# A hybrid diffusion layer on one core: gate rows on ScalarE's queue, deferred statistics, separate PSUM pools, earlier loads of w_down, later output stores

## The chip, the cores and the metric

The kernel runs on one core of a Trainium2 chip. The metric is the device time of one execution in microseconds, the median of several. A core has TensorE (PE: matmuls, with its weight loads listed apart as PEld), VectorE (DVE), ScalarE (ACT), GpSimd (POOL) and SyncE (SP), which computes nothing and issues DMAs. ACT and POOL can issue DMAs too. Every engine executes its own list of instructions strictly in order; an instruction that waits holds up everything behind it on its engine. Waits are on semaphores that other engines or finished DMAs raise.

## What is computed

One layer of a network: 128 context tokens and 2048 latent tokens of width 1024 pass a gated short convolution and a bidirectional mLSTM scan in chunks of 128 tokens, then a feed-forward part with a convolution, all in float32.

```python
def trunk_layer(x, mod, ...):
    h = rmsnorm(x, norm1) * (1 + scale1) + shift1
    z = h @ w_in
    sc_b, sc_c, sc_x, q, k, v, o, g = jnp.split(z, idx, axis=-1)
    u = (sc_c * sc_x).reshape(B, rows, row_len, D_CONV)
    y_sc = sc_b * conv3(u, conv_sc_w, conv_sc_b, axis=2).reshape(B, T, D_CONV)
    h_m, C, n, m = mlstm_bidir(heads(q), heads(k), heads(v), gates, C0, n0, m0)
    h_m = h_m * lax.rsqrt(jnp.mean(h_m * h_m, axis=-1, keepdims=True) + EPS)
    ...
    x = x + gate1 * (jnp.concatenate([y_sc, h_m], axis=-1) @ w_out)
    h2 = rmsnorm(x, norm2) * (1 + scale2) + shift2
    up = (h2 @ w_up).reshape(B, rows, row_len, 2 * D_FF)
    up = conv3(up, conv_ffn_w, conv_ffn_b, axis=ffn_axis).reshape(B, T, 2 * D_FF)
    a, gg = jnp.split(up, 2, axis=-1)
    x = x + gate2 * ((jax.nn.silu(gg) * a) @ w_down)
    return x, C, n, m
...
y_prompt = rmsnorm(xp, final_norm)
y_sample = rmsnorm(xs, final_norm)
```

## The kernel before

Tokens stand in the columns of every tile, features in the partitions. A float32 product is made of three matmuls of split operands: each matrix is a rounded high part and the rest (`wh`, `wl` for weights, `hH`, `hL` or `tH`, `tL` for activations), and `wh*hH + wh*hL + wl*hH` is summed in PSUM. ACT makes the high parts, DVE the low ones. The tokens of the first half are six blocks of 384 or 256 columns in three groups, (0,1), (2,3) and (4,5). `gemm` (L201) makes one 128-row piece of a product for one block: 8 x 3 matmuls into a PSUM tile `acc`.

The program runs through these stages. Python generators (`chain`, `run`, `islice`) decide which piece of side work is emitted between which two gemms; the framework then fixes the order of every engine's list and puts in the waits.

- The modulation vectors and the products with `w_in` (to about 640 us). Beside them `prep_down` (L576) forms sums of the blocks of `w_down` for a seven-product (Strassen-like) scheme: a lot of 512 or 384 columns is two loads `wm` (L586), four DVE operations (L601 to L604) and four stores to `wD` (L606). There are 12 lots. All three tiles of a lot come from one ring of five buffers, `wm`.
- The gates, then two passes of `weave` (L908) over the mLSTM units with gemms between them. A `Mix` unit is a chunk and a pair of heads: `load` (L828) fetches k, v, q, o, `sb` and the gate rows `R` (L834, one row of `nD` broadcast to all partitions, 512 KB, four buffers); `first` (L842) makes the scores S on PE (L845), adds a mask to R on DVE (L846), takes the exponential on ACT (L850) and multiplies with S on DVE (L854); `second` (L857) makes y on PE (L868, L870), from it `hv` on DVE, and squares it on ACT (`sj`, L887); `third` (L893) transposes hv on PE into the PSUM tile `st` (L897), scales it on DVE (o, L899) and stores it to `yD` (L902). There are 34 units. At step i of `weave` unit i runs `first`, unit i-3 `third`, unit i-1 `second`, and unit i+2 is loaded. Between two units lie one or two gemms.
- In the second pass these gemms are the short convolution (L418 to L439) and the output projection `out_proj` (L446): per group and per m of eight, weights `wst` (L109), rows of x (L466), a gemm for either block, the residual `row` on DVE (L483), its store to `xD` (L485), squares `sq` on ACT (L492) and their sum on DVE (L493). After a group its `stats` (L441) run: `inv_rms` (L124) multiplies the squares with ones on PE (L128, into a tile of the same pool `st`), and DVE (rc, L131) and POOL (L132) make 1/rms of it.
- `sums` applies the second norm to a pair of blocks (F, L234 to L253, tD). The third group's `out_proj` (`last`, L957) is run in between.
- The products with `w_up` in the seven-product scheme (PE L1143 to L1145, to about 2190 us), with PSUM tiles of three kinds, a, b and c, from one pool `pu` (L969); then those with `w_down` (PE L1201 to L1203). Their weights are loaded into `st` (L285, L294, L328). Finished blocks of the output are normed: `norm` (L1081) makes the 1/rms, spreads it, scales eight tiles (DVE L1091), stores them (`out_y`, L1093 for the second half of the tokens, L1095 for the first) and loads the next half's residual into the same tiles (L1060).

Nearly all DMAs are issued by SP (`Q` in the code), among them all those named here. `S` is ACT, `V` DVE, `G` POOL.

## Time and profile before

| | us |
|---|---|
| median of 3 runs | 2519.47 (2518.98 to 2521.13) |
| the profiled execution | 2520.55 |
| its span in the trace | 2518.8 |
| PE busy | 2464.3 (98%) |
| DVE busy | 1740.9 (69%) |
| ACT busy | 1100.6 (44%) |
| POOL busy | 67.0 (3%) |
| DMA, mean over the span | 201 GB/s |

The profile lists, for every instruction, its start, its duration and how long its engine stood idle before it, with the instruction or DMA that ended this idle time. A matmul's listed duration is longer than the step from one to the next, since they are pipelined. PEclk is the granted clock of TensorE: 1.00 in a stretch is its full level, 2.4 GHz, and 0.5 the lower one, 1.2 GHz. Times of the trace count from the start of the span.

### The profile page before, as it was taken

How to read it: one execution, taken by the hardware profiler on the slowest of the kernel's cores; microseconds unless marked ns; L12 is line 12 of the kernel's file. 1: busy time of each engine (PE TensorE's matmuls, PEld its weight loads, DVE VectorE, ACT ScalarE, POOL GpSimd, SP SyncE). 2: the span in 40 equal slices, each digit the busy share in tenths (PEclk: the TensorE clock that was granted, in tenths of full speed). 3: DMA queues.
4: the chain of work that ended last, by engine and by line, in shares of the span. 5: the costliest groups of instructions: out<-in, count | busy, mean ns of one | idle time of the engine just before them, and what ended most of it. 6: DMA issues, size and time to landing. Idle time of an engine off the chain costs nothing.

```text
span 2518.8 us, 46131 instructions
## 1 busy us (share of the span) xinstructions
PE 2464.3 (98%) x17967; PEld 2446.1 (97%) x17967; DVE 1740.9 (69%) x3401; ACT 1100.6 (44%) x2109; POOL 67.0 (3%) x130
## 2 busy tenths in 40 slices
PE   8999999999999989999999999999999999999998
PEld 8999999999999989999999999999999999999998
DVE  4995443343467767889798879776767787677665
ACT  4521143333344444555454446544545543443343
POOL 0000000000011110000000000000000000000000
PEclk9999999999999999999999999999999999999999
DMA  8888733466567886977456446544444485576544
GB/s 287 281 278 268 224 102 105 140 205 211 175 199 205 256 272 199 291 249 250 149 198 210 151 158 229 186 155 157 149 163 143 158 299 202 189 241 221 181 158 145
DMA packets 252445, 506.29 MB, mean 201 GB/s; under 512 B 22963, under 2 KB 153155, under 8 KB 241347
## 3 DMA queue, kind: packets, MB, share of 16 engines
q1 hardware_dynamic: 252226, 503.35, 60.5%
q8 instruction: 141, 2.31, 0.4%
q14 instruction: 78, 0.63, 0.1%
HBM read 355.24 MB, written 148.03 MB: 200 GB/s over the span
## 4 chain that ended last, share of the span: by engine, by line
PE 77%; DVE 9%; DMA 9%; issue 2%; ACT 2%; SPq 1%; POOL 0%; DVEq 0%; ACTq 0%; POOLq 0%
PE pa L1143 7%; PE pa L1145 7%; PE pa L1144 7%; PE acc L206 5%; PE acc L208 5%; PE acc L207 5%; PE pb L1145 3%; PE pb L1143 3%; PE pb L1144 3%; DVE jk L555 3%; PE pa L1203 2%; PE pa L1201 2%; PE pa L1202 2%; DMA wD<-wm 2%; DMA R<-nD 2%; PE pc L1144 2%
## 5 line engine op out<-in xcount | busy, mean ns | idle before, releaser
L206 PE MATMUL acc<-hH,wh 128*128 128x384 f32 (+1 forms) x1536 | 513.7, 334 | 5.5 <-DVE cr L425 3.0
L208 PE MATMUL acc<-hH,wl 128*128 128x384 f32 (+1 forms) x1536 | 504.9, 329 | 0.0
L207 PE MATMUL acc<-hL,wh 128*128 128x384 f32 (+1 forms) x1536 | 504.2, 328 | 0.0
L1143 PE MATMUL pa<-tH,wh 128*128 128x272 f32 x1408 | 409.2, 291 | 4.1 <-DVE row L483 2.9
L1145 PE MATMUL pa<-tH,wl 128*128 128x272 f32 x1408 | 407.9, 290 | 0.0
L1144 PE MATMUL pa<-tL,wh 128*128 128x272 f32 x1408 | 405.9, 288 | 0.0
L278 ACT ACTIVATE wh<-st 128x512 fp32r<-128x512 f32 (+1 forms) x312 | 188.7, 609 | 418.9 <-PE pa L1144 118.2
L206 PEld LDWEIGHTS acc<-hH,wh 128*128 128x128 f32 x1536 | 290.3, 189 | 7.5 <-DVE cr L425 3.4
L207 PEld LDWEIGHTS acc<-hL,wh 128*128 128x128 f32 x1536 | 290.1, 189 | 0.7
L208 PEld LDWEIGHTS acc<-hH,wl 128*128 128x128 f32 x1536 | 290.1, 189 | 0.3 <-issue 0.2
L984 DVE SCALAR_TENSOR_TENSOR tt<-raw,fw,tt 128x127 f32<-128x127 f32 (+4 forms) x264 | 242.2, 947 | 47.3 <-ACT tt L990 46.2
L279 DVE TENSOR_TENSOR wl<-st,wh 128x512 fp32r<-128x512 f32 (+1 forms) x312 | 205.4, 660 | 98.8 <-ACT wh L278 93.3
L1143 PEld LDWEIGHTS pa<-tH,wh 128*128 128x128 f32 x1408 | 265.7, 189 | 5.1 <-DVE row L483 3.1
L1144 PEld LDWEIGHTS pa<-tL,wh 128*128 128x128 f32 x1408 | 266.1, 189 | 0.0
L1145 PEld LDWEIGHTS pa<-tH,wl 128*128 128x128 f32 x1408 | 265.4, 189 | 0.0
L1143 PE MATMUL pb<-tH,wh 128*128 128x272 f32 x704 | 203.6, 289 | 0.4 <-ACT wh L278 0.4
L1145 PE MATMUL pb<-tH,wl 128*128 128x272 f32 x704 | 203.6, 289 | 0.0
L1144 PE MATMUL pb<-tL,wh 128*128 128x272 f32 x704 | 202.7, 288 | 0.0
L278 ACT ACTIVATE wh<-s 128x512 fp32r<-128x512 f32 x176 | 110.9, 630 | 148.1 <-PE pc L1144 90.5
L1203 PE MATMUL pa<-tH,wl 128*128 128x256 f32 (+1 forms) x528 | 152.6, 289 | 0.2 <-DVE wl L279 0.2
L1201 PE MATMUL pa<-tH,wh 128*128 128x256 f32 (+1 forms) x528 | 152.8, 289 | 0.0
L1202 PE MATMUL pa<-tL,wh 128*128 128x256 f32 (+1 forms) x528 | 152.4, 289 | 0.0
(236 smaller groups left out, 5485.3 us busy)
## 6 DMA issues: line engine op xcount, KB each, us to landing
st<-in_w_up SPq DMA_DIRECT2D x88, 512.0 KB, 4.5
wst<-in_w_in SPq DMA_DIRECT2D x48, 512.0 KB, 4.2
wU<-s SPq DMA_DIRECT2D x22, 1024.0 KB, 6.6
s<-wU SPq DMA_DIRECT2D x22, 1024.0 KB, 5.7
st<-wD SPq DMA_DIRECT2D x32, 704.0 KB, 4.9
st<-in_w_down SPq DMA_DIRECT2D x28, 704.0 KB, 4.1
R<-nD SPq DMA_DIRECT2D x34, 512.0 KB, 5.6
wm<-in_w_modr SPq DMA_DIRECT2D x32, 512.0 KB, 4.9
```

What stands on the lines that cost most here:

```text
L206: PE.matmul(acc[:, :n], w_h, hH[:, k, :n], start=(k == 0), stop=False)
L207: PE.matmul(acc[:, :n], w_h, hL[:, k, :n], start=False, stop=False)
L208: PE.matmul(acc[:, :n], w_l, hH[:, k, :n], start=False, stop=(k == KT - 1))
L278: S.activation(wh[:, :n], a, AF.Copy)
L279: V.tensor_sub(wl[:, :n], a, wh[:, :n].bitcast(F32))
L984: V.scalar_tensor_tensor(o, i, w, o, op0=ALU.mult, op1=ALU.add)
L1143: PE.matmul(acc, wh[:, w], rh, start=(kk == 0 and i in (0, 1, 5)), stop=False, skip_group_check=True)
L1144: PE.matmul(acc, wh[:, w], rl, start=False, stop=False, skip_group_check=True)
L1145: mm = PE.matmul(acc, wl[:, w], rh, start=False, stop=(kk == 3), skip_group_check=True)
L1201: PE.matmul(acc[p], wh[:, k], th[:, t], start=(c == kk == 0), stop=False, skip_group_check=True)
L1202: PE.matmul(acc[p], wh[:, k], tl[:, t], start=False, stop=False, skip_group_check=True)
L1203: PE.matmul(acc[p], wl[:, k], th[:, t], start=False, stop=(c == 2 and kk == nk - 1), skip_group_check=True)
```

## The change

There are five edits.

1. `Mix.load` issues R on ACT's DMA queue (`S.dma_start`) and not on SP's.
2. `out_proj` no longer runs a group's `stats` at its end. It puts them into a list `late`, from which the next group's `out_proj` takes them after its first gemm of m = 1, tied behind that gemm's last matmul (`latest`). Those of the last group still run beside the first products with `w_up`. In connection with this the last group runs four gemms, not one, ahead of the second part of `sums`.
3. The products with `w_up` and `w_down` take their PSUM tiles from three pools, c, b and a, not from one.
4. `prep_down` loads a lot ahead of the one whose sums it makes, and the tile of the sums has a ring `ws` of its own (2 buffers) beside `wm` (5).
5. `norm` stores a tile of the output, and reloads it, when two more have been scaled. For the second half's first block the two half stores of a tile become one.

```diff
@@ gemm
+    latest, late = [], []
...
-            PE.matmul(acc[:, :n], w_l, hH[:, k, :n], start=False, stop=(k == KT - 1))
+            mm = PE.matmul(acc[:, :n], w_l, hH[:, k, :n], start=False, stop=(k == KT - 1))
+        latest[:] = [mm]
@@ out_proj
                         acc = gemm(w, y, n)
+                        if m == 1 and b == grp[0] and late:
+                            with tc.issue_after(latest[0].ins):
+                                late.pop()()
...
-                if grp is grps[-1] and defer is not None:
-                    defer.append(lambda: stats(grp, sss))
-                else:
-                    stats(grp, sss)
+                late.append(lambda grp=grp, sss=sss: stats(grp, sss))
@@ prep_down
-                for mp, c0, n in lots:
-                    a, b = load(mp, c0, n)
+                nxt = load(*lots[0])
+                yield
+                for x, (mp, c0, n) in enumerate(lots):
+                    a, b = nxt
+                    if x + 1 < len(lots):
+                        nxt = load(*lots[x + 1])
                     store()
                     yield
                     a11, a12, a21, a22 = a[:, 0], a[:, 1], b[:, 0], b[:, 1]
-                    s = stp.tile([P, 1024], F32, name="wm", bufs=5).rearrange("p (k c) -> p k c", k=2)[:, :, :n]
+                    s = stp.tile([P, 1024], F32, name="ws", bufs=2).rearrange("p (k c) -> p k c", k=2)[:, :, :n]
@@ Mix.load
-                Q.dma_start(self.R.rearrange("p h k d t -> p (h k d t)"),
+                S.dma_start(self.R.rearrange("p h k d t -> p (h k d t)"),
                             nD[r0:r0 + 2].rearrange("h k d t -> (h k d t)")[None, :].to_broadcast([P, 1024]))
@@ the last group
-        late = []
-        last = out_proj(((4, 5),), late)
-        run(islice(last, 1))
+        last = out_proj(((4, 5),))
+        run(islice(last, 4))
@@ the products
-        pu = ph2.enter_context(tc.tile_pool(name="pu", bufs=2, space=PSUM))
+        pu = {k: ph2.enter_context(tc.tile_pool(name="p" + k, bufs=n, space=PSUM)) for k, n in (("c", 2), ("b", 2), ("a", 3))}
...
-            return pu.tile([P, 512], F32, name="p" + kind, bufs=3 if kind == "a" else 2)
+            return pu[kind].tile([P, 512], F32, name="p" + kind)
@@ norm
+            due = []
             for m in range(KT):
                 q = outs[m, blk][:, p * n:(p + 1) * n]
                 V.scalar_tensor_tensor(q, q, nrm[:, 2, m:m + 1], rb[:, :n], op0=ALU.mult, op1=ALU.mult)
-                if hf:
+                if then is None:
                     Q.dma_start(O["y"][m][:, t0 + p * n:t0 + (p + 1) * n], q)
-                elif p:
-                    Q.dma_start(O["y"][m][:, t0:t0 + 2 * n], outs[m, blk])
-                    then(m)
+                    continue
+                if p:
+                    due.append((m, outs[m, blk]))
                 if m % 2:
                     yield
+                    while len(due) > (2 if m < KT - 1 else 0):
+                        m1, o = due.pop(0)
+                        Q.dma_start(O["y"][m1][:, t0:t0 + 2 * n], o)
+                        then(m1)
```

In the order of the instructions this looks as follows. Line numbers of the changed kernel are up to 11 higher than those of the kernel before.

SP's list before, around the R load of one of the last units. `row` is a row of x for the residual, `k`, `q`, `v`, `o` and `sb` are the loads of `Mix`, `yD` is the store of `third`:

```order
L765 DMA q_10001<-qD 128x2x128 [waits DMAHW2_49]
L466 DMA row<-in_x 128x384 [waits DMAHW5_49,DMAHW3_49,Activation_49]
L902 DMA yD<-o_9511 128x2x128 [waits DMAHW4_49,DVE_49]
L834 DMA R<-nD 128x1024 [waits PE_49]
L770 DMA v_9999<-vD 128x258 [waits DMAHW6_49]
L765 DMA o_9961<-oD 128x2x128 [waits DMAHW7_49,DMAHW4_49]
L838 DMA sb<-sD 128x516 [waits DMAHW0_49,DVE_49]
```

ACT's list in the changed kernel around two of these loads (L857 is the exponential, L894 and L898 are `sj` and the scaling of hv, L111 makes a high part of `w_out`, L498 squares):

```order
L841 DMA R<-nD 128x1024 [waits DMAHW1_49,PE_49]
L894 ACTIVATE sj,hss<-hv 128x128 [waits DVE_49] x2
L898 ACTIVATE hv<-hv,hss 128x128 [waits Activation_49,Pool_49]
L898 ACTIVATE hv<-hv,hss 128x128 [waits Activation_49]
L111 ACTIVATE wh<-wst 128x1024 [waits PE_49]
L498 ACTIVATE sq<-row 128x384 [waits DVE_49]
L857 ACTIVATE R<-R,cols 128x128 [waits DMAHW1_49]
L857 ACTIVATE R<-R,cols 128x128 x3
L498 ACTIVATE sq<-row 128x384 [waits DMAHW2_49,DVE_49]
L841 DMA R<-nD 128x1024 [waits DMAHW6_49,PE_49]
```

The R load has left SP's list, where it stood behind the store of o, and stands on ACT behind the exponential of the unit before and ahead of `sj`.

PE's list before at the statistics of group (0,1), directly behind the y of a unit:

```order
L870 MATMUL y<-v_9654,R 128x129
L868 MATMUL y<-sb,qs 128x129
L870 MATMUL y<-v_9654,R 128x129
L128 MATMUL st<-ones,ss 128x1 [waits DVE_49]
L128 MATMUL st<-ones,ss 128x1 x2
L206 MATMUL acc<-hH,wh 128x384
L207 MATMUL acc<-hL,wh 128x384
```

PE's list in the changed kernel at the same statistics:

```order
L210 MATMUL acc<-hH,wl 128x384
L128 MATMUL st<-ones,ss 128x1 [waits DVE_49]
L128 MATMUL st<-ones,ss 128x1 x2
L208 MATMUL acc<-hH,wh 128x384
L209 MATMUL acc<-hL,wh 128x384
L210 MATMUL acc<-hH,wl 128x384
L208 MATMUL acc<-hH,wh 128x384
L128 MATMUL st<-ones,ss 128x1 [waits DVE_49]
L128 MATMUL st<-ones,ss 128x1 x2
L209 MATMUL acc<-hL,wh 128x384
```

DVE's list before at the two `rc` that read these statistics (`st` has one buffer, so the second block's `inv_rms` needs the first block's `rc` done):

```order
L493 TENSOR_TENSOR ss<-ss,sq 128x384 [waits Activation_49]
L877 TENSOR_SCALAR hv<-y,den 128x128 [waits DVE_49]
L131 TENSOR_SCALAR rc<-st 128x3 [waits PE_49,Pool_49]
L878 SCALAR_TENSOR_TENSOR hv<-y,den,hv 128x128 [waits DVE_49]
L131 TENSOR_SCALAR rc<-st 128x3 [waits PE_49,Pool_49]
```

DVE's list in the changed kernel there (L853 is the mask of a later unit):

```order
L885 SCALAR_TENSOR_TENSOR hv<-y,den,hv 128x128 [waits DVE_49]
L114 TENSOR_TENSOR wl<-wst,wh 128x512
L853 TENSOR_TENSOR R<-R,maskN 128x2x256 [waits DMAHW6_49]
L131 TENSOR_SCALAR rc<-st 128x3 [waits PE_49,Pool_49]
L489 SCALAR_TENSOR_TENSOR row<-acc,modT,row 128x384
L131 TENSOR_SCALAR rc<-st 128x3 [waits PE_49,Pool_49]
```

On PE the first block's statistics have moved behind a whole gemm; the second block's now stand four matmuls behind the first block's, where before they stood 15 matmuls behind. On DVE a low part of weights and a mask, which waits for its R to land, have come to stand ahead of the first `rc`.

SP's list before at the norm of the first half's second block, from its last store of the output to the next weights and activations:

```order
L1095 DMA out_y<-o_23312 128x512 [waits DVE_49]
L1060 DMA o_25930<-xD 128x576 [waits DMAHW7_49,DMAHW3_49]
L1060 DMA o_25934<-xD 128x576 [waits DMAHW4_49,DMAHW0_49]
L1060 DMA o_25938<-xD 128x576 [waits DMAHW5_49,DMAHW1_49]
L1060 DMA o_25942<-xD 128x576 [waits DMAHW6_49,DMAHW2_49]
L328 DMA st<-in_w_down 128x1408 [waits Activation_49]
L328 DMA st<-in_w_down 128x1408 [waits DVE_49]
```

The same place in the changed kernel:

```order
L1108 DMA out_y<-o_23318 128x512 [waits DVE_49]
L1066 DMA o_25967<-xD 128x576 [waits DMAHW7_49,DMAHW3_49]
L1066 DMA o_25970<-xD 128x576 [waits DMAHW4_49,DMAHW0_49]
L1066 DMA o_25973<-xD 128x576 [waits DMAHW5_49,DMAHW1_49]
L1066 DMA o_25976<-xD 128x576 [waits DMAHW6_49,DMAHW2_49]
L331 DMA st<-in_w_down 128x1408 [waits Activation_49]
L331 DMA st<-in_w_down 128x1408 [waits DVE_49]
```

Here nothing has moved: four stores, four loads, four stores, four loads and two loads of weights stand in this order in both lists. At the norm of the first block a load of weights has moved from behind six stores to behind two.

## Rows read from the trace of the kernel before

**Rows 1.** The page, busy time of each engine, share of the span, and instructions.
```profile
PE 2464.3 (98%) x17967; PEld 2446.1 (97%) x17967; DVE 1740.9 (69%) x3401; ACT 1100.6 (44%) x2109; POOL 67.0 (3%) x130
```

**Rows 2.** Whom PE waited for, whole span: us in total, times, longest us.
```profile
PE S L845 <- DVE R L854: 8.0, 3, 4.5
...
PE st L128 <- DVE o L899: 4.1, 1, 4.1
PE pb L1201 <- ACT wh L278: 3.2, 1, 3.2
PE acc L206 <- DVE cr L425: 3.0, 2, 1.5
PE pa L1143 <- DVE row L483: 2.9, 1, 2.9
...
PE acc L206 <- DVE yr L438: 2.6, 1, 2.6
```

**Rows 3.** Five stretches: length, busy engines, PEclk, DMA share, GB/s.
```profile
258.00:268.00 10.00, 7.72 (x35) 7.72 (x36) 4.65 (x9) 0.60 (x1) 0.00 (x0) 0.83 0.86 287
892.00:902.00 10.00, 6.12 (x35) 6.12 (x36) 8.64 (x26) 3.64 (x11) 0.51 (x1) 0.83 0.93 309
930.00:942.00 12.00, 7.92 (x38) 7.72 (x37) 8.03 (x28) 5.29 (x17) 2.60 (x4) 0.72 0.87 267
1080.00:1090.00 10.00, 7.69 (x49) 7.70 (x50) 5.77 (x8) 4.60 (x8) 0.00 (x0) 0.83 0.96 320
2285.00:2295.00 10.00, 6.81 (x41) 6.76 (x41) 5.42 (x9) 3.56 (x6) 0.00 (x0) 0.83 0.85 307
```

**Rows 4.** Whom DVE waited for, 195 to 293 us: total, times, longest.
```profile
DVE wm L601 <- DMA wD<-wm: 36.9, 9, 7.2
```

**Rows 5.** Timeline of DVE in prep_down: start, duration, operation, idle before, releaser.
```profile
251.44 0.69 DVE L601 TENSOR_TENSOR wm<-wm 128x512 f32<-128x512 f32 x1 [4.11 <-DMA wD<-wm]
...
258.61 0.56 DVE L601 TENSOR_TENSOR wm<-wm 128x384 f32<-128x384 f32 x1 [2.04 <-DMA wD<-wm]
```

**Rows 6.** Timeline of PE at a Mix unit.
```profile
859.62 0.33 PE L207 MATMUL acc<-hL,wh 128*128 128x384 f32 x1
859.79 0.34 PE L208 MATMUL acc<-hH,wl 128*128 128x384 f32 x1
862.27 0.71 PE L845 MATMUL S<-q,k 128*128 128x128 f32 x4 [2.14 <-DVE R L854]
...
865.26 0.42 PE L206 MATMUL acc<-hH,wh 128*128 128x384 f32 x1
```

**Rows 7.** Timeline of SP, two of the R loads.
```profile
872.46 0.48 SPq L834 DMA_DIRECT2D R<-nD  x1
...
918.19 0.46 SPq L834 DMA_DIRECT2D R<-nD  x1
```

**Rows 8.** Timeline of DVE, two masks that waited for R.
```profile
891.00 0.69 DVE L846 TENSOR_TENSOR R<-R,maskN 128x512 f32<-128x512 f32 x1 [4.63 <-DMA R<-nD]
...
923.46 0.69 DVE L846 TENSOR_TENSOR R<-R,maskN 128x512 f32<-128x512 f32 x1 [5.09 <-DMA R<-nD]
```

**Rows 9.** Instructions of tile R, 846 to 930 us: min, median, max ns.
```profile
L850 ACT ACTIVATE R<-R,cols x34: 384/387/403, 845.8 to 925.6; 128x128 f32<-128x128 f32 x34
```

**Rows 10.** Whom ACT waited for, 640 to 936 us: total, times, longest.
```profile
ACT hH L456 <- DMA xt<-yD: 17.0, 5, 4.1
```

**Rows 11.** Timeline of DVE before the first product with w_up.
```profile
1079.57 0.62 DVE L483 SCALAR_TENSOR_TENSOR row<-acc,modT,row 128x384 f32<-128x384 f32 x1 [2.63 <-DMA row<-in_x]
...
1081.78 0.48 DVE L483 SCALAR_TENSOR_TENSOR row<-acc,modT,row 128x256 f32<-128x256 f32 x1
```

**Rows 12.** Timeline of SP, loads of rows of x.
```profile
1073.99 1.71 SPq L466 DMA_DIRECT2D row<-in_x  x2
```

**Rows 13.** Timeline of SP at the second output block: loads of weights.
```profile
2280.47 0.90 SPq L328 DMA_DIRECT2D st<-in_w_down  x2
```

**Rows 14.** Timeline of ACT at the second output block.
```profile
2287.56 1.56 ACT L278 ACTIVATE wh<-st 128x512 fp32r<-128x512 f32 x3 [3.42 <-DMA st<-in_w_down]
```

8 lines of the change are left out of this document (4 added, 4 removed).

## The prediction

> **What bounds the kernel now.** I read the busy times first: PE works 2464.3 us of the span, DVE, the next, 1740.9 [rows 1]. So PE sets the end, and only two things can be won: time in which PE stands, and time in which it runs at the lower clock. The list of whom PE waited for comes next [rows 2]; apart from the start and the tail of the program its longest entries are those that answer to the five edits. The third view is the granted clock behind such waits [rows 3]. In ten microseconds a mean of 0.83 means that (1 - 0.83) x 10 = 1.7 us of full-speed work were lost: in these stretches PE has stood, and then runs at 1.2 GHz (0.5) for a while before it has 2.4 GHz again. The stretch with 0.72 loses 0.28 x 12 = 3.4, but it begins ahead of a wait of 4.1 us, and part of the low clock passes while PE stands; I count 2.5, an estimate. A wait therefore costs its length and a tail:
>
> - A, sums of w_down: 3.0 + 2.6 + 1.7 = 7.3 us.
> - B, gate rows R: 8.0 + 1.7 = 9.7 us.
> - C, statistics: 4.1 + 2.5 = 6.6 us.
> - D, first product with w_up: 2.9 + 1.7 = 4.6 us.
> - E, weights behind the output's stores: 3.2 + 1.7 = 4.9 us.
>
> Together 33.1 us, 1.3% of the time, are within reach. The rest of PE's waits the change does not touch.
>
> **A, a lot ahead.** DVE stands 36.9 us in nine waits ahead of the first sum of a lot [rows 4], and the convolution's operations behind it, for which PE waits, come late by that. Two lots follow each other after 7.2 us [rows 5], waits of 4.11 and 2.04 included. PE's step from matmul to matmul is 0.17 us [rows 6]; two gemms, 48 matmuls, take 8.2, and a lot is due for about two gemms. So the transfers can nearly keep up and the lateness is one of order: load, sums and store in a circle through the five buffers. With a lot loaded ahead and the sums in buffers of their own, the store of the sums is out of the circle. What is left of it: one of the two loads still needs a buffer that an earlier lot's store frees. DMA was 86% busy in the first of the five stretches [rows 3], and the bytes are the same; that is what may keep a wait. Bounds: 1.5 us, if only the last lot's wait goes, which no other lot pushes, and 7.3, if all goes. I take 5.0.
>
> **B, R on ACT's queue.** The loop is: mask (DVE), exponential (ACT), product (DVE), for whose PSUM tile PE's next S waits. The mask comes 5.3 us after SP issues R: 918.19 to 923.46 [rows 7, 8]. Of these it stands 5.09 waiting [rows 8], so R was issued too late by all of it. Why late: the unit whose S starts at 862.27 [rows 6] makes its y until the next gemm begins at 865.26 [rows 6], which frees a buffer, and the R that takes it is issued at 872.46 [rows 7], 7 us later. SP stood in that time at other loads and stores ahead in its list. On ACT the load stands behind the exponential of the unit before, 4 x 0.39 = 1.6 us [rows 9], and perhaps a square. The new loop is mask 0.69, exponential 1.6, issue 0.46, landing 5.3: 8.1 us, with a square some 8.6, against two gemms (8.2) and a unit's own matmuls (3.0 from 862.27 to 865.26, some of it waits; I take 2.5), 10.7 us. The wait should go. Against it: ACT too stands at loads, 17.0 us in five waits for xt, up to 4.1 each [rows 10], and R stands behind some of them. Adding 3.4 to 8.4 gives 11.8, over 10.7 by 1.1 us, in up to five units. I take 2.2 us as kept, 7.5 as gained; bounds 3.0 (kept: five times 1.1, and a tail of the clock of 1.7) and 9.7. The issues themselves, 34 x 0.47 = 16 us, go from SP to ACT, whose busy time is 1100.6 of 2518.8 [rows 1]; they lie beside PE's gemms. Behind them on ACT stand `sj` and the high parts of w_out, which have a gemm to spare.
>
> The row says that R lands 5.3 us after its issue and is issued 7 us late. The Trainium skill, "DMA: Bandwidth & Descriptors", section "Issuing engines are not separate DMA queues", says that DMAs issued by different engines share the same 16 DMA engines, so that several issuers save only the sequencer's time to issue. Read strictly this speaks against the edit: by it R lands no sooner, and only its issue is saved. That is the second rival below. I hold that what SP costs here is not its issuing but the waits in its list, of which the rule says nothing.
>
> **C, statistics.** PE's `st<-ones` waited 4.1 us for o on DVE [rows 2], since `st` is one buffer and o still had to read the transposed hv. Behind a gemm (24 x 0.17 = 4.1 us) o is long done, and the wait goes, with its tail. New is the second block's: four matmuls (0.7 us) later it needs `rc` of the first on DVE, and ahead of `rc` now stands a mask that waits for the last R. If this R is in time, `rc` comes about as PE arrives. If it waits as the masks do now, PE stands up to 5.1 us [rows 8] and 1.7 in the tail, and nothing is won: bounds -0.2 and 6.6. With R earlier (B) I take 5.0. The same pattern recurs for the second group, without R ahead of it.
>
> **D, three PSUM pools.** The first product waited 2.9 us [rows 2] for the last but one and the last `row`, which end at 1080.2 and 1082.3 and were themselves held by 2.63 us of waiting for rows of x [rows 11], loaded from 1073.99 on [rows 12]. With a pool of its own the first product takes a bank that y left long ago, and needs no `row`. Next late would be the second product: its activations go from tD over ACT to DVE, and DVE's low part stands behind the first of these two `row`. PE is through with the first product, 24 matmuls of 272 columns, 3.0 us after its start, which is 1082.3 - 2.9 = 1079.4 without the wait (an estimate from 0.17 us for 384 columns [rows 6]); even a `row` that ends at 1080.2 leaves DVE time for it. In the new order the loads of x also stand ahead of w_up's on SP, so the 2.63 us should go too. Against it: sums for later products have come nearer to the end of the gemms on DVE. Four operations as long as `row` (0.62 us) put ahead of the low part make it 2.5 us late; PE then stands about 1.9 of the 2.9 us, and the tail stays. Bounds: 1.0 by that, and 6.0 (the 4.6 and some 1.4 of small waits behind it). I take 3.8.
>
> **E, stores two scalings behind.** PE waited 3.2 us for a high part that itself waited 3.42 us for its load [rows 14], issued at 2280.47 [rows 13] behind eight stores and eight loads. That is the second block, and there SP's order is word for word the same as before; the edit moves a load of weights only at the first block, behind which PE does not wait. So nothing is won at this place: 0, bounds -1.0 and 1.0 for what the moved issues shift. The eight stores saved in the second half lie on SP while PE computes: 0.
>
> **Sum.** 5.0 + 7.5 + 5.0 + 3.8 + 0 = 21.3 us. From the profiled 2520.55 that leaves 2499.3. That run is 1.1 above the median of those shown (2519.47), so 2498.2 in the median; I say 2498.
>
> **The rivals.**
> 1. *R stays late, now on ACT.* For it: the waits for xt [rows 10], and DMA 93% busy in the second stretch [rows 3], so that R may land later. Then B keeps two thirds of its loss and gives 3.0, the last mask holds `rc`, and C gives 1.0; A 3.5, D 2.5. Sum 10: 2510.5, in the median 2509.4. Against it: the loop of some 8.4 us.
> 2. *Only the issue is saved.* Each R comes 0.46 us earlier; the loss falls on some seven units, so B gives 7 x 0.46 = 3.2, the rest as forecast: 17.0, in the median 2502.5. The rule above would have it so; the 7 us between free buffer and issue [rows 6, 7] speak against it.
> 3. *The waits only change places.* PE's gemms between units then meet the next late thing (weights of w_out, rows of x), A stays bound by DMA at 86%, and less than 5 us remains: 2515 to 2523. Against it: five places hundreds of microseconds apart would all have to fail.
> 4. *ACT becomes the late engine: slower.* R on ACT waits until y has freed its buffer, and behind it ACT holds the high parts of the next weights. If the landing of R, and what stands behind it, falls one ACT wait (3.4 us, 17.0 / 5) later in ten of the units, PE loses 10 x 3.4 = 34 us against the 9.7 it lost there, C is not won, and A and D give 8.8: 2520.55 + 24.3 - 8.8 = 2536, in the median 2535. It decides from the point where R is issued on ACT later than the 7 us behind y that SP took. Against it: ACT is busy 44%.
>
> That an edit does not do what it says is part of the forecast already (E).
>
> **How the numbers follow.** Chances: forecast 0.62 (2490 to 2508), rival 1 0.16, rival 2 0.09, rival 3 0.08, rival 4 0.05. The bounds of the terms give 4.3 and 30.6 us together, that is 2515.2 and 2488.8; all at one end at once is unlikely, and above lies rival 3. I set the range at 2487 to 2514, which leaves out rival 4, rival 3, and some 5 in a hundred of the rest. A measurement of this kernel can tell about 0.2% (5 us) from no change. Faster by more: forecast and rivals 1 and 2, 0.87. Within: rival 3, 0.08. Slower: rival 4, 0.05.
>
> **What would show it.** A: no DVE wait for wD over 4 us between 195 and 293 us, and no PE wait for cr or yr. B: the entry "S waits for DVE's product" below 2.5 us, masks with waits under 1 us, R issued on ACT within 3 us of y. C: no wait of PE for o at the statistics; a wait for `rc` there, if any, below 1.5 us. D: the first product without a wait, the second with less than 1 us. E: the wait of about 3 us for the high part of w_down still there. I am wrong if PE's waits for S or for `rc` are as long as now, if E has gone (then the order was not what held the load), or if PE waits at places where it did not before.

## The result, and the profile after

The changed kernel is slower: 2532.35 us median (2528.71 to 2537.78) against 2520.3 us (2517.67 to 2525.35) in the same comparison, a ratio of 1.0046 with a 95% interval of 1.0033 to 1.0059, some 11.6 us. The forecast was 2498, and its range ended at 2514. The profiled execution is the longest of the six (2537.78 us, span 2535.9), so of the 17 us by which its trace is longer than that of before (span 2518.8), some 5 belong to this execution and not to the change.

The instructions are the same, 17967 on PE, and so nearly are the busy times: PE 2472.2 us against 2464.3, DVE 1742.2 against 1740.9 [rows 1]. So of the 17.1 us between the two spans PE is busy for 7.9 with the same matmuls, at a lower mean clock (0.987 against 0.992), and stands for 9.2.

Whom PE waited for in after, whole span: us in total, times, longest us. It answers to [rows 2].

```profile
PE st L128 <- DVE rc L131: 12.2, 3, 11.1
...
PE S L852 <- DVE R L861: 6.4, 3, 4.6
PE st L139 <- POOL fr L132: 6.1, 3, 4.2
PE acc L208 <- DVE yr L441: 5.5, 2, 2.8
...
PE pb L1212 <- ACT wh L281: 2.4, 1, 2.4
```

Four of the five places are there again. The wait for o has gone, and in its place `st` waits 11.1 us for `rc`. The waits for cr and yr (3.0 + 2.6 before) are 5.5 for yr alone. S waits 6.4 instead of 8.0. The wait for `row` has gone (D). The high part of w_down at the second output block still waits, 2.4 and 1.0 more in a smaller entry (E), and new is `fr`, 4.2 us, at the first output block, where the longest of these waits was 1.1.

Behind the waits the clock is low. Two stretches of after (length, busy engines, PEclk, DMA share, GB/s), to be held against [rows 3]:

```profile
946.00:966.00 20.00, 8.95 (x43) 8.63 (x42) 9.56 (x29) 8.73 (x26) 2.85 (x4) 0.66 0.70 220
1094.00:1114.00 20.00, 16.68 (x102) 15.65 (x101) 13.93 (x20) 12.52 (x19) 1.89 (x2) 0.83 0.84 286
```

In the stretch of the `rc` wait PE is busy for 9 of 20 us, and the lower clock takes (1 - 0.66) x 20 = 6.8 us, partly while PE stands. At the first products with w_up, where the wait for `row` has gone, 0.17 x 20 = 3.4 us are lost to the clock; before, 20 us from 1080 on had 0.91 and lost 1.8.

A second reading needs no list of waits. From the first S of the `Mix` units to the last gemm of the output stage (`acc`) PE does the same 2,700 matmuls in every kernel of this study. Instructions by line, min, median, max ns, first and last start; before, then after:

```profile
L845 PE MATMUL S<-q,k x136: 270/275/582, 648.4 to 975.4; 128*128 128x128 f32 x136
```
```profile
L208 PE MATMUL acc<-hH,wl x1536: 279/334/528, 96.5 to 1079.1; 128*128 128x384 f32 x160, 128*128 128x256 f32 x32
```
```profile
L852 PE MATMUL S<-q,k x136: 270/275/582, 651.3 to 985.4; 128*128 128x128 f32 x136
```
```profile
L210 PE MATMUL acc<-hH,wl x1536: 274/334/525, 99.1 to 1088.8; 128*128 128x384 f32 x160, 128*128 128x256 f32 x32
```

This stage takes 1079.1 - 648.4 = 430.7 us before and 1088.8 - 651.3 = 437.5 after. So of the 17.1 us between the two spans 2.9 lie ahead of it, 6.8 in it and 7.4 behind it.

**The 11.1 us for `rc`.** Rows of the timeline of after, each engine's in turn (start, duration, operation, idle before, releaser):

```profile
948.58 0.42 SPq L457 DMA_DIRECT2D xt<-yD  x1
955.13 0.94 ACT L459 ACTIVATE hH<-xt 128x384 fp32r<-128x384 f32 x2 [9.60 <-DMA xt<-yD]
955.57 0.33 ACTq L841 DMA_DIRECT2D R<-nD  x1
957.56 1.04 ACT L111 ACTIVATE wh<-wst 128x1024 fp32r<-128x1024 f32 x1
958.63 0.69 DVE L114 TENSOR_TENSOR wl<-wst,wh 128x512 fp32r<-128x512 f32 x1 [8.41 <-ACT wh L111]
...
960.10 0.69 DVE L853 TENSOR_TENSOR R<-R,maskN 128x512 f32<-128x512 f32 x1
960.71 0.15 DVE L131 TENSOR_SCALAR rc<-st 128x3 f32<-128x3 f32 x1
960.92 1.44 PE L128 MATMUL st<-ones,ss 128*128 128x1 f32 x6 [11.05 <-DVE rc L131]
```

Read upwards: PE waits for `rc`, a row of 0.15 us. Ahead of it on DVE stands the mask, and it has no wait of its own: R is there. Ahead of the mask stands the low part `wl` of a weight of w_out, which waits 8.41 us for ACT's high part; and that stands on ACT behind `hH`, which waits 9.60 us for a transfer `xt`, issued at 948.58. One transfer holds four operations on three engines.

Two things more stand in this trace. First, PE has no use yet for what holds the row: a block has eight hH, and these are the 33rd to 36th of 48, the first half of the third group's first block. PE begins that block's first gemm at about 1029, 74 us later. Second, the R whose mask stands ahead of `rc` went out from ACT at 955.57 only, behind the hH, and its mask began 4.5 us later. R takes a median of 5.2 us to land in this trace, so without `wl` the mask could hardly have come sooner; x_rcfirst, below, shows it.

**The 4.2 us for `fr`.** Rows of the timeline of after at the first output block, each engine's in turn:

```profile
2248.82 2.65 SPq L1108 DMA_DIRECT2D out_y<-o  x2
2255.12 0.95 SPq L1066 DMA_DIRECT2D o<-xD  x2
2256.60 0.42 SPq L1048 DMA_DIRECT2D F<-uD  x1
2266.23 2.22 ACT L1054 ACTIVATE tH<-F 128x1152 fp32r<-128x1152 f32 x2 [2.11 <-DMA F<-uD]
2267.43 2.63 DVE L1055 TENSOR_TENSOR tL<-F,tH 128x1152 fp32r<-128x1152 f32 x2 [2.59 <-ACT tH L1054]
...
2272.51 1.91 POOL L132 TENSOR_TENSOR fr<-fr,mhalf 128x2 f32<-128x2 f32 x1 [37.74 <-DVE fr L131]
2274.48 1.22 PE L139 MATMUL st<-ident,fr 128*128 128x128 f32 x4 [4.20 <-POOL fr L132]
```

The last two stores, held back by the edit, stand ahead of two loads of o, which wait for them to land; behind those stand the loads of F, and behind F come the activations on ACT, their low parts on DVE, and at last `fr`.

### The profile page after: what moved, and what is told of

It is laid out like the page before. It is cut to its first block, busy times and chain, and to the rows that moved or that the text cites. A ratio compares the mean times of both kernels' runs of the same rounds, so it can differ in the third digit from the quotient of the medians.

```text
span 2535.9 us, 46121 instructions
## 1 busy us (share of the span) xinstructions
PE 2472.2 (97%) x17967; PEld 2452.8 (97%) x17967; DVE 1742.2 (69%) x3401; ACT 1100.3 (43%) x2109; POOL 66.4 (3%) x130
## 5 line engine op out<-in xcount | busy, mean ns | idle before, releaser
L114 DVE TENSOR_TENSOR wl<-wst,wh 128x512 fp32r<-128x512 f32 (+1 forms) x160 | 106.1, 687 | 70.6 <-ACT wh L111 70.4
```

## The experiments

Each ratio is to the kernel before, run on the same chip in the same rounds, with a 95% interval. Edits are counted as in the list of the change, with the prediction's letters: 1 the gate loads R on ACT (B), 2 statistics held back (C), 3 PSUM pools by kind with the four steps of the last group that belong to them (D), 4 sums one lot ahead (A), 5 stores two scalings behind (E).

### One edit taken out

u_stats, edit 2 undone, u_norm, edit 5, u_R, edit 1, u_prep, edit 4 (each the lines of the change put back):

```diff
u_stats   -                late.append(lambda grp=grp, sss=sss: stats(grp, sss))
          +                    stats(grp, sss)
u_norm    -                    due.append((m, outs[m, blk]))
          +                    Q.dma_start(O["y"][m][:, t0:t0 + 2 * n], outs[m, blk])
          +                    then(m)
u_R       -                S.dma_start(self.R.rearrange("p h k d t -> p (h k d t)"),
          +                Q.dma_start(self.R.rearrange("p h k d t -> p (h k d t)"),
u_prep    -                        nxt = load(*lots[x + 1])
          +                    a, b = load(mp, c0, n)
```

> The changed kernel with edit 2 undone alone: the statistics of groups (0,1) and (2,3) run at the group's end again, the other four edits stay. Theory S (the held-back statistics cost the time: rc stands on DVE behind a low part of w_out whose high part stands on ACT behind hH, which waits for xt): PE's wait of 11.1 us for rc goes, with about 2.5 us of low clock; a wait for o of up to 4 us with its tail comes back. The time falls by about 7 us, from 12 us over the kernel before to about 5 over it. Theory N (the held-back stores of the norm cost it): no change, 12 us over. Theory R (loading R from ACT holds ACT up): no change of the time, the wait only gets another name.

> The changed kernel with edit 5 undone alone: every output tile is stored and reloaded when it is scaled, as before. Theory N: the wait of 4.2 us of the spread for POOL's 1/rms of the second block shrinks to about 1 us, its low clock of 3 us goes, and the time falls by about 6 us, to 6 over the kernel before; the wait of 2.4 us for the high part of w_down (pb) stays. Theory S: the wait of 11 us for rc stays as it is; both may hold at once. If neither: 12 us over, and the 4.2 us stay.

> The changed kernel with edit 1 undone alone: R is loaded by SP's queue again. Theory R: ACT no longer stands at R, PE's wait for rc falls from 11 us to below 4, and the time falls by 7 us or more. Theory S (hH waiting for xt is what holds ACT, not R): the wait for rc stays at 8 us or more, and PE's waits for S rise from 6.4 us to about 8; the time is 11 to 14 us over the kernel before.

> The changed kernel with edit 4 undone alone: a lot of w_down is loaded when the one before is summed, all tiles in one ring of five. The prediction held that edit 4 gains 5 us; then this runs 5 us slower than the changed kernel, 17 over the kernel before. By the trace of the changed kernel DVE's waits for a lot went only from 36.9 to 32.1 us and PE's waits there from 5.6 to 5.5 us: then no change within 2 us. If the lot ahead fills the DMA queues for others (87% busy from 195 to 295 us, 80% before), this is faster by 2 to 3 us.

Measured against 1.0046 for all five edits: u_stats 2527.93, 1.0022 [1.0008, 1.0036]; u_norm 2529.19, 1.003 [1.0018, 1.0042]; u_R 2526.38, 1.0014 [1.0001, 1.0027]; u_prep 2532.8, 1.0042 [1.0025, 1.0058]. Whom PE waited for, u_stats, then u_R:

```profile
PE st L128 <- DVE o L903: 3.5, 1, 3.5
```
```profile
PE S L852 <- DVE R L861: 7.7, 3, 3.5
PE st L128 <- DVE rc L131: 6.9, 2, 6.6
```

With the statistics back in their old place the 11 us for `rc` are gone (0.9 is left) and the 3.5 for o are back. With R back on SP, `rc` still waits 6.6 us, so R's queue isn't what makes it wait, though it adds to it. Edit 4 changes nothing that can be measured: 0.04%, and the two intervals together leave 0.2% either way. Edits 2, 5 and 1 undone give back 0.24, 0.16 and 0.32%. The first and the last are clear of the noise of such a difference, just under 0.2%; the 0.16 of edit 5 isn't. The three sum to more than the 0.46% there is, but with this noise it isn't shown that what they cost overlaps.

### What holds `rc`

x_onest: the sums of both blocks go into one PSUM tile, so that the second block's matmuls need no `rc` of the first.

```diff
-            for b, ss in zip(grp, sss):
-                inv_rms(ss, BL[b][1], rcol(b))
+            ps, i = pst.tile([P, 512], F32, name="st"), 0
+            for b, ss in zip(grp, sss):
+                for k in range(BL[b][1] // P):
+                    PE.matmul(ps[:, i:i + 1], ss[:, k * P:(k + 1) * P], ones[:, 0:1], start=True, stop=True)
+                    i += 1
...
```

> The changed kernel, with the statistics of both blocks of a group in six columns of one st tile, so that the second block's sums need no rc of the first. Theory S (the place of rc behind the low part, with one st buffer, is the cause): PE's wait of 11 us goes and with it about 2.5 us of low clock; the time falls by 10 to 13 us, to that of the kernel before. Theory H (DVE and ACT stand there behind hH, which waits for xt, whoever asks first): PE runs on for one gemm (4 us) and then waits about 7 us at S or at the transposes of the next unit; the time falls by about 4 us, to 7 to 8 over the kernel before.

Measured: 2522.18, 1.0022 [1.0008, 1.0035]. Rows of its timeline:

```profile
945.41 0.94 ACT L468 ACTIVATE hH<-xt 128x384 fp32r<-128x384 f32 x2 [8.65 <-DMA xt<-yD]
948.91 0.69 DVE L114 TENSOR_TENSOR wl<-wst,wh 128x512 fp32r<-128x512 f32 x1 [8.01 <-ACT wh L111]
951.35 0.66 PE L913 MATMUL st<-ident,hv 128*128 128x128 f32 x2 [5.27 <-DVE rc L454]
```

ACT's wait for xt and DVE's behind it are as long as before; PE has one more piece of work ahead and then stands 5.27 us for the same `rc`. About half of the wait is bought off, not its cause.

x_rcfirst: the fourth weight of a group is loaded one product later, and its low part stands behind `rc` on DVE.

```diff
-                    if m + 2 < KT:
+                    if m + 2 < KT and m != 1:
                         ws.append(load_w(I["w_out"][m + 2]))
...
+                        if m == 1 and b == grp[0]:
+                            with tc.issue_after(read[0].ins):
+                                ws.append(load_w(I["w_out"][3]))
```

> The changed kernel, with the fourth weight of each output group loaded one product later and its low part put behind the statistics on VectorE: in VectorE's row the two wl stand behind both rc, and in their old place ahead of the first rc stand two hL of the second block, which wait for ScalarE's hH and so for the same transfer xt. Theory that what holds rc is the transfer xt (ScalarE's hH waits 8 to 10 us for it, and all else stands behind): TensorE's wait for rc at the second output group stays at 6 us or more, time within 0.15% of the changed kernel. Theory that the weight's low part held it (ScalarE's wh, the weight's own load): the wait falls under 3 us and the time by 5 to 8 us, to about 2525.

Measured: 2532.9, 1.0045 [1.0028, 1.0063]. Its timeline:

```profile
951.75 0.52 ACT L461 ACTIVATE hH<-xt 128x384 fp32r<-128x384 f32 x1 [6.17 <-DMA xt<-yD]
951.82 0.33 ACTq L846 DMA_DIRECT2D R<-nD  x1
952.31 0.56 DVE L462 TENSOR_TENSOR hL<-xt,hH 128x384 fp32r<-128x384 f32 x1 [4.92 <-ACT hH L461]
...
955.80 0.69 DVE L858 TENSOR_TENSOR R<-R,maskN 128x512 f32<-128x512 f32 x1 [1.73 <-DMA R<-nD]
956.61 1.44 PE L130 MATMUL st<-ones,ss 128*128 128x1 f32 x6 [6.55 <-DVE rc L133]
```

Now `hL` stands ahead of `rc` and waits for the same xt, and behind `hL` the mask waits 1.73 us more for its R, which ACT issued at 951.82, behind the same hH. PE's wait is 6.55, over the 6 that the theory of the transfer gave, and the time is that of the changed kernel; PE's waits for S have grown from 6.4 to 10.0. So the weight was only the last member of the row. The transfer xt held it, in two ways: over DVE's low parts, and over the R that stands behind hH on ACT.

### One edit alone

s_R has edit 1 alone, s_stats edit 2, s_pools edit 3, s_norm edit 5.

```diff
s_R       -                Q.dma_start(self.R.rearrange("p h k d t -> p (h k d t)"),
          +                S.dma_start(self.R.rearrange("p h k d t -> p (h k d t)"),
s_stats   -                    stats(grp, sss)
          +                late.append(lambda grp=grp, sss=sss: stats(grp, sss))
s_pools   -            return pu.tile([P, 512], F32, name="p" + kind, bufs=3 if kind == "a" else 2)
          +            return pu[kind].tile([P, 512], F32, name="p" + kind)
s_norm    -                    Q.dma_start(O["y"][m][:, t0:t0 + 2 * n], outs[m, blk])
          -                    then(m)
          +                    due.append((m, outs[m, blk]))
```

> The kernel before with edit 1 alone: R loaded by ACT's queue. The prediction gave it 7.5 us. By the runs so far (masks waited 46 us for R instead of 53, PE's waits for S went from 8.0 to 6.4 us, undoing it in the changed kernel gained about 8 us) it gains nothing: 0 to 4 us slower than the kernel before, waits of PE for S of 5 to 7 us whose last link is the low part of w_out (wl) behind hH, and not the mask.

> The kernel before with edit 2 alone: the statistics held back until after the next group's first gemm of m = 1, R still on SP. Theory S: PE's wait for o of 4.1 us goes and a wait for rc of 6 to 11 us comes; 3 to 7 us slower than the kernel before. If the stall in the changed kernel needs R on ACT as well (undoing R took it from 11.2 to 6.7 us): the wait is below 4 us and the time that of the kernel before within 2 us. The prediction had 5 us faster.

> The kernel before with edit 3 alone, with the four gemms ahead of the second part of sums: the prediction gave it 3.8 us. PE's wait of 2.9 us for the row goes. If small waits for high and low parts of the activations and for the spread take its place as in the changed kernel (1.2 + 1.0 + 0.9 + 0.9 us and two low clocks of 1.6): 0 to 1 us gained; if those came only with the other edits: 3 to 4 us.

> The kernel before with the stores of the first output block two scalings behind, alone. Theory that the last stores, now later, hold the next loads on SyncE's queue: TensorE waits 3 to 5 us for fr near 2255 us where it waited 1 us, and the time rises by 3 to 5 us, ratio 1.001 to 1.002. The prediction's value: nothing, 0.9996 to 1.0004. Theory that the wait only comes with the other edits (their earlier start changes the order): no fr wait over 2 us, ratio 1.000.

Measured: s_R 2526.17, 1.0031 [1.0016, 1.0047]; s_stats 2519.6, 1.0001 [0.9991, 1.001]; s_pools 2519.73, 1.0002 [0.9986, 1.0018]; s_norm 2522.61, 1.0006 [0.9993, 1.0019]. (In s_stats the sums of the feed-forward's input read the second group's 1/rms before it is written, since without edit 3 only one step of the last group runs ahead of them. So it leaves out a wait; v_all_but below has the edit with this wait, together with edits 3 and 4.) R on ACT is the one edit that loses by itself. Held-back statistics alone gain nothing and lose nothing: the wait for o has gone and 3.6 us for `rc` stand in its place. s_norm has the new wait at the first output block,

```profile
2257.04 0.71 PE L139 MATMUL st<-ident,fr 128*128 128x128 f32 x4 [4.01 <-POOL fr L132]
```

as long as in the changed kernel, but its price of 3 to 5 us isn't seen in the medians; the interval allows up to 0.19% (4.8 us), so it isn't excluded either. In the traces with edit 5 the longest wait for `fr` is between 1.6 and 4.2 us, in those without it between 1.1 and 2.5, so the 4 us are not constant.

### What R on another engine costs

y_nostats_nonorm is the changed kernel with edits 2 and 5 undone; y_prep_pools has edit 1 undone as well. The two differ in one word, `S` or `Q` before the load of R.

> The changed kernel with two edits undone: the statistics of the output stage stand where they stood before, and so do the stores of the first output block. ScalarE's gate loads, the PSUM pools and the sums one lot ahead stay. Theory of the two stalls: the loss of about 12 us is TensorE's wait of 11.2 us for rc (about 6 more than the waits of before in the same stretch) and its new wait of 4.2 us for fr at the first output block; with both gone nothing is left, ratio 0.999 to 1.001 (2518 to 2523 against 2520), and ScalarE's loads cost nothing. Theory of the gate loads: their move alone measured 1.003, so they cost 7 to 8 us by themselves wherever they stand, ratio 1.002 to 1.004, with no single wait over 6 us to show for it. Both expect no TensorE wait for rc over 1 us at the second output group, an o wait of about 3.6 us back at 926 us, and no wait for fr over 2 us near 2255 us.

> The kernel before with the sums one lot ahead and the PSUM pools by kind, and nothing else of the change. The prediction's prices for the two were gains of 5.0 and 3.8 us: it expects 0.9965, about 2511.5 against 2520, with no VectorE wait for the sums' loads over 4 us. Theory that a wait only changes place (the load's wait takes the store's, 32 of 37 us; small waits replace the row wait): 0.9985 to 1.0015, waits of VectorE for the loads of w_down at 30 us or more in sum, TensorE's loss between 180 and 295 us within 2 us of before. Against the kernel without the two other edits it differs by the gate loads alone: the theory of the two stalls expects the two within 0.15%, the theory of the gate loads expects this one faster by 0.2 to 0.4%.

Measured: y_nostats_nonorm 2527.6, 1.0028 [1.0014, 1.0042]; y_prep_pools 2523.63, 1.0003 [0.9992, 1.0014]. With both stalls undone the loss is still 0.28%, and it goes with R. The theory that the two stalls are the loss has fallen. And sums a lot ahead with PSUM pools, priced at 8.8 us together, gain nothing that is seen; the interval leaves 2 us at most. At the unit whose S is due near 865 us, timeline of y_nostats_nonorm (R on ACT), then y_prep_pools (R on SP):

```profile
861.62 0.94 ACT L456 ACTIVATE hH<-xt 128x384 fp32r<-128x384 f32 x2 [6.19 <-DMA xt<-yD]
...
869.59 0.34 ACTq L838 DMA_DIRECT2D R<-nD  x1
870.14 1.23 PE L849 MATMUL S<-q,k 128*128 128x128 f32 x4 [5.47 <-DVE R L858]
```
```profile
864.85 0.71 PE L849 MATMUL S<-q,k 128*128 128x128 f32 x4 [2.50 <-DVE R L858]
...
866.67 0.48 SPq L838 DMA_DIRECT2D R<-nD  x1
867.89 1.77 ACT L456 ACTIVATE hH<-xt 128x384 fp32r<-128x384 f32 x4 [3.14 <-DMA xt<-yD]
```

With R on ACT two of the four hH stand ahead of the unit's work and wait 6.19 us; the next R goes out at 869.59, 17.0 us after the last (852.55), and S waits 5.47 in one piece. With R on SP hH stands behind, R follows R after 12.6 us (854.03, 866.67), and S waits 2.50 here and again at later units.

Does R's place in ACT's row cost? z_Rpool issues R from POOL, before otherwise; s_R_again is s_R once more, on the same chip.

```diff
-                Q.dma_start(self.R.rearrange("p h k d t -> p (h k d t)"),
+                G.dma_start(self.R.rearrange("p h k d t -> p (h k d t)"),
```

> The kernel before with the gate loads R issued by GpSimd instead of SyncE, nothing else. SyncE's row is but for three loads the same as with R on ScalarE alone (which measured 1.0031), TensorE's is the same as before; what differs from that kernel is only that R no longer stands in ScalarE's row. Theory that R in ScalarE's row costs (ScalarE's hH waits 6 us for xt at one unit, and the next R is issued only behind it: 17 us from one R to the next where it was 12 to 13): the interval comes back to 11 to 14 us, the TensorE wait for S of 5.5 us at that unit is split or gone, ratio 0.999 to 1.001. Theory that SyncE without R runs ahead and its xt and weight loads now fall together with R: the loss stays, ratio 1.002 to 1.004, xt takes 8 us or more from issue to landing and ScalarE's hH still waits 5 us or more. Prediction's price: with R off SyncE up to 7.5 us gained, 0.997.

> The kernel before with the gate loads on ScalarE alone, a second time, on the same chip as the one with GpSimd. Theory of R in ScalarE's row: 1.002 to 1.0045 again, with one R interval of 16 to 18 us between 845 and 870 us, and a TensorE wait for S of 5 us or more there. If the 1.0031 was an accident of that chip: 0.999 to 1.001.

Measured: z_Rpool 2527.38, 1.0039 [1.0023, 1.0055]; s_R_again 2523.53, 1.0019 [1.0005, 1.0032]. POOL loses at least as much, and my theory of ACT's row has fallen too. Timeline of z_Rpool, with the y that frees a buffer at 874.64 and the R that takes it:

```profile
859.90 0.94 ACT L456 ACTIVATE hH<-xt 128x384 fp32r<-128x384 f32 x2 [5.68 <-DMA xt<-yD]
...
869.55 1.23 PE L845 MATMUL S<-q,k 128*128 128x128 f32 x4 [5.07 <-DVE R L854]
...
874.00 0.64 PE L870 MATMUL y<-v,R 128*128 128x129 f32 x2
875.07 0.60 POOL L834 DMA_DIRECT2D R<-nD  x1
...
959.01 0.94 ACT L456 ACTIVATE hH<-xt 128x384 fp32r<-128x384 f32 x2 [19.45 <-DMA xt<-yD]
971.14 1.22 PE L845 MATMUL S<-q,k 128*128 128x128 f32 x4 [12.10 <-DVE R L854]
```

The same hH waits as long with R on POOL, and a later one 19.45 us, with S behind it at 12.10. And R is not late there. An R takes the buffer of the unit four before it. From the end of the y that frees it to the issue of R the median of the last 13 loads, those beside the output projection, is 7.0 us before, 2.7 in s_R, 3.7 in after and 0.4 in z_Rpool. R went out sooner in every kernel that moved it, and no such kernel was faster. What is common to both is that R has left SP's list and xt and its hH have come forward: the first xt of the second group goes out at 859.3 before, at 838.2 in s_R and at 842.8 in z_Rpool, though PE begins that group only between 932 and 941.

z_R_later_half leaves R on ACT and takes up the second half of xt, with its hH and hL, one step of the weaving later.

```diff
                     for kh in range(2):
+                        if kh:
+                            yield
                         yt = xp.tile([P, 4, 384], F32, name="xt")
```

> The kernel before with the gate loads on ScalarE and the second half of each output block's transfer xt, with its four hH and hL, taken up one step of the weaving later. In ScalarE's row hH then stands behind the exponentials of the unit at hand instead of ahead of its sums of squares. Theory that R's move costs because hH and its xt come forward in the rows and hold ScalarE (6 us at one unit, S waits 5.5 us in one piece, next R 17 us after the last): that wait of ScalarE for xt near 860 us falls under 3 us, no TensorE wait for S over 4 us there, R intervals under 14 us, ratio 0.999 to 1.001. If it is R's issue from another engine as such, or the sum of waits moves elsewhere: 1.002 to 1.004 still.

Measured: 2532.01, 1.005 [1.0032, 1.0068], no faster than s_R. Its waits, PE's, then ACT's:

```profile
PE S L847 <- DVE R L856: 14.0, 4, 6.6
```
```profile
ACT hH L458 <- DMA xt<-yD: 12.8, 6, 5.1
```

ACT's waits for xt are half (12.8 against 23.4 in the trace of s_R_again), and the one near 860 us is gone, but S now waits at two other units, 14.0 in all. So this wait was not the loss either; it was where the loss showed in those orders.

What does show is the time. All eleven kernels without R on SP have an interval above 1 (from 1.0005 up); of the six others only u_R has (from 1.0001). And it shows in the stage, last gemm minus first S, the same matmuls, in us:

| R issued by | kernels | stage |
|---|---|---|
| SP | s_norm, s_pools, y_prep_pools, before, v_all_but, u_R, s_stats | 426.1, 426.7, 429.5, 430.7, 430.7, 433.7, 437.8 |
| ACT or POOL | u_stats, x_onest, s_R, y_nostats_nonorm, s_R_again, u_norm, x_rcfirst, after, z_Rpool, u_prep, z_R_later_half | 431.3, 431.6, 435.3, 435.3, 435.5, 435.8, 436.8, 437.5, 439.9, 441.8, 442.2 |

The means are 430.7 and 436.6: some 6 us, about the 0.2 to 0.3% of the ratios. The two lists overlap, and their kernels differ in more than R. But the pairs that differ in R's issue alone say the same: before to s_R and s_R_again 4.6 and 4.8 us longer, u_R to after 3.8, y_prep_pools to y_nostats_nonorm 5.8, before to z_Rpool 9.2. So the move of R is shown to cost; how the time is lost there differs from order to order, and why every order without R on SP is worse stays open.

### What is left without edits 1 and 5

v_all_but: edits 2 (with one PSUM tile, as in x_onest), 3 and 4 on the kernel before.

> The kernel before with the statistics held back (both blocks in one PSUM tile), the PSUM pools by kind and the sums one lot ahead; without the two edits that cost, the gate loads on ScalarE and the held-back stores. If the prediction's prices for these three had held beside each other (5.0, 5.0, 3.8), 0.9945, about 2506. Theory that each wait only changes place: 0.9985 to 1.001. Theory that held-back statistics cost even so, since rc stands behind ScalarE's hH and its xt: 1.001 to 1.0025, with a TensorE wait of 5 us or more for rc or behind it at the second output group.

Measured: 2520.29, 1.0002 [0.999, 1.0014]. The forecast gains of 13.8 us are not there; the interval leaves 2.5. In its trace PE waits for S for 4.0 and 2.0 us, 2.8 for `rb` at 1031, and 2.3 in two waits at the first products with w_up. No version beats the kernel before.

## Why the prediction was wrong

**The sum took five waits as five losses.** It named the wait, priced it with its tail and let it go. The runs show that an edit that removes the wait (o, `row`, the store of the sums) leaves the time where it was: 1.0001, 1.0002 and 1.0003 for edits 2, 3, and 3 with 4. Rival 3, at 0.08, is what these edits do; the 2515 to 2523 that it gave fit each single edit that doesn't touch R.

The tail was no fixed price either. PE waits 2.7 us for `rb` in s_stats, and the clock then takes 6.8 us (0.73 and 0.59 in the 20 us from 1030); it waits 2.8 for the same in v_all_but, and the clock takes 1.7 (0.83 from 1030 to 1040). In s_norm the wait for `row` is there, 2.77, and PEclk is 1.00 from 1070 to 1100. The 1.7 to 2.5 of each term were read rightly from the one trace of before, but they don't come with every such wait.

**A, taken 5.0, measured nothing.** The step that failed is that, with the store of the sums "out of the circle", most of the wait goes: the prediction itself named the load that still needs a buffer, and then bounded what it keeps at 5.8 of 7.3 and took 2.3. Timeline of after, SP's then DVE's:

```profile
245.20 0.90 SPq L589 DMA_DIRECT2D wm<-in_w_down  x2
...
249.92 0.69 DVE L608 TENSOR_TENSOR ws<-wm 128x512 f32<-128x512 f32 x1 [6.02 <-DMA wm<-in_w_down]
```

DVE now waits for the load, where it waited 36.9 us for the store [rows 4]. Whom DVE waited for, 195 to 293 us of after:

```profile
DVE ws L608 <- DMA wm<-in_w_down: 30.9, 8, 6.0
```

From 190 to 300 us all its waits for the lots' loads and stores are 37.5 us, where they were 45.5; PE's waits for cr and yr there are 5.5, where they were 5.6. So DVE stands 8 us less, and PE as long as before.

**B, taken 7.5, measured a loss of 5 to 8 us.** What it said of R held: R was late on SP, and the longest S of before, 4.5 us at 895.88, stands behind a mask that waited 4.63 for R [rows 8]. From another queue R went out sooner, 3.7 us behind the y that freed its buffer where it was 7.0. The step that failed is "The wait should go", that with R early nothing else holds S. Against it the prediction set only "R stands behind some of the waits for xt; I take 2.2 as kept", which sizes R's own delay. What stands behind hH on ACT is also the high part, behind that the low part on DVE, behind that the product that S waits for. Timeline of after, the place of [rows 6]:

```profile
860.77 0.94 ACT L459 ACTIVATE hH<-xt 128x384 fp32r<-128x384 f32 x2 [5.29 <-DMA xt<-yD]
...
864.82 0.69 DVE L114 TENSOR_TENSOR wl<-wst,wh 128x512 fp32r<-128x512 f32 x1 [2.90 <-ACT wh L111]
869.29 1.22 PE L852 MATMUL S<-q,k 128*128 128x128 f32 x4 [4.55 <-DVE R L861]
```

The run from POOL shows it most plainly: R goes out 0.4 us behind the y, and S waits 20.0 us in three waits, the longest behind an hH that waits 19.45 for xt. That this is the whole of the loss isn't shown; z_R_later_half took one such wait away and lost as much. Nor do the masks' waits for R tell the kernels apart: 49.0 to 63.0 us with R on SP, 50.1 to 60.3 with R elsewhere.

Rival 2 took the rule of the Trainium skill, "DMA: Bandwidth & Descriptors", section "Issuing engines are not separate DMA queues". The traces agree with it on the transfer: R lands in a median of 5.6 us before, from SP, 5.2 in after, from ACT, and 5.5 in z_Rpool. I set it aside for the 7 us between free buffer and issue, and there the rows are on my side, R's issue moved by more than its own 0.46 us. But neither the larger gain nor the 3.2 us that the rival left was there, for the reason above. Rival 4 had the sign and ACT as the late engine, and its 2535 is the number nearest to the measured 2532, by luck: R left ACT sooner behind y than it had left SP, its price of 34 us was three times the whole loss, it counted 8.8 of gains that didn't come, and the run from POOL shows that R in ACT's row is not the mechanism.

**C, bounds -0.2 to 6.6, measured 11.1 us of waiting where 4.1 were.** The step that failed is the list of what stands ahead of `rc`: the prediction named the mask and its R, and bounded the wait by the mask's 5.1. In the trace the mask has no wait; ahead of it stand `wl`, `wh` and hH with 9.6 us for xt. The bound was taken from one engine's row; DVE's row has a second wait, and its releaser waits too. The mask alone would have held `rc` as well, since its R stood behind the same hH on ACT: so far rival 1, "the last mask holds `rc`", was right. Undoing the edit gives 0.24% back, alone it costs nothing. The longest wait of hH for xt is 4.1 us before, 5.5 with edit 2 alone, 6.2 with R on ACT alone, and 7.2 to 9.7 with edit 2 and three or four of the others: among the five edits it takes several together to make it long, and the held-back statistics turn that into PE's wait. ACT's waits for xt as a whole are 23.3 us before and 23.4 after; they lie in fewer pieces.

**D, taken 3.8, measured nothing.** The mechanism was right, the first product waits no more for `row`. The size was not. In the 40 us behind the last gemm PE waits 4.0 us before, 2.9 of them for `row`, and 3.1 in after, 3.2 in s_pools: small waits took the place, the largest 0.94 for tL and 0.85 for `rc`. And in after the clock lost 3.4 us in the 20 around them instead of 1.8. The interval of edit 3 alone would still allow a gain of 3.5 us, the one with edit 4 only 2.

**E, taken 0 within 1.** Right that the second block keeps its wait (2.4 and 1.0, was 3.2). Wrong that PE doesn't wait behind the first block's loads: `fr` waited 4.2. The order had shown the moved load, and I looked for a wait at that load alone, not for what stands behind it three engines on. What the 4 us cost in time isn't clear of noise: 0.16% given back in u_norm, 0.06% lost in s_norm.

**The range and chances.** It was said that I am wrong if waits for `rc` are as long or PE waits at new places; both happened. The chance of 0.05 for slower rested on one mechanism, R late on ACT. That five edits to rows already in balance could each make something else late was not given a chance of its own.

## What to carry to other kernels

Before an operation is put behind another in an in-order row, follow not only what stands ahead of it there, but what each of those waits for, engine by engine, to the transfer at the end; the bound of the new wait is that transfer's, not the nearest row's. Ask too when the work that stands there is due: here ACT stood at a high part that PE needed 74 us later, with work behind it that was due at once. Where PE's waits are 2% in all and spread over many rows that a planner sets, a wait that is taken away mostly reappears: price such an edit by trying it alone, and expect nothing until a stage of equal work gets shorter. Moving a load to another engine's queue can send it out sooner, but it also changes every row that the planner builds from it, and that can cost more than it saves.

## What the runs showed that was not expected

Single executions of the kernel before spread from 2509.78 to 2529.84 us on one chip, and a trace can be 5 us off its median, so a list of waits from one trace can't carry a claim of 3 us; the time of a stage of equal work, over seven and eleven traces, could. R's move costs the same few microseconds from a queue that is nearly idle (POOL, 67 us busy) as from ACT's. A transfer xt of 768 KB took 9.1 us from issue to landing in y_nostats_nonorm, where it went out within a microsecond of R and a weight, and about 6 us in y_prep_pools, where neither went out with it (issued 861.88, hH at 867.89).
